# Reordering the head of a hybrid attention layer: constants on a second queue, the modulation row spread by products, other filler products

## The chip, the cores and the metric

The kernel runs on one core of one Trainium2 chip. The metric is the device time of one execution in microseconds (us); less is better. The core has a matrix engine (PE, with its weight loads shown as PEld), a vector engine (DVE), an activation engine (ACT), a small general engine (POOL) and a queue engine (SP) that issues most transfers. ACT can issue transfers too.

## The reference

One layer of a decoder with 512 positions, width 1024 and heads of 64. What matters here is its beginning:

```
mod = silu(c) @ w_ada + b_ada ;  shift, scale, gate = split(mod, 3)
h    = rms_norm(x, norm_gain) * (1 + scale) + shift
proj = h @ w_in                      # q, k, v, z of two head groups
...                                  # sliding-window group A, three-branch sparse group B
out  = x + gate * (y @ w_out)
```

`c` is one vector of 1024, `x` is 512 x 1024. The row sums of `x*x` give one factor for each position; `silu(c) @ w_ada` gives a scale and a shift for each of the 1024 channels. Both are wanted before the first product `h @ w_in`.

## The kernel before, in words

`x` lies transposed in eight tiles `xT[k]` of 128 channels by 512 positions. For each tile k the kernel needs the two columns `AB[:, k, :]` (scale and shift of its 128 channels) and the positions' factor spread over the partitions (`rbp` in PSUM, `rb` in SBUF). Then `h = A*(xT*rb) + B` is made as a high part `hh` and a low part `hl` (rounded value and remainder), the weights `w_qkv_a` of the tile likewise (`swh`, `swl`), and `first_proj(k, n)` (L281) adds three products, n = 0, 1, 2: hh by swh, hh by swl, hl by swh. Each is eight matmuls, so a tile is 24, all adding to the same six PSUM banks `sq` and `skv`.

The scale and shift come in two ways. For tiles 0 and 1 (`PE_MODS`) the matrix engine makes them: `mod_pe(k)` (L225) multiplies the columns of `w_ada` by `scz`, which holds silu(c) by column; ACT copies the result to `macc`, `mod_col(k)` (L246) sums it over the partitions by two one-column products with `ones`, and `mod_ab(k)` (L252) adds the constants on DVE. For tiles 2 to 7 the vector engine makes them: `mod_rows(k)` (L219) multiplies the rows of `w_ada` by `scrow`, silu(c) spread over all partitions, and sums along the row: two instructions of 1024 elements for a tile.

The order of the head is written by hand. Everything from L290 to L413 stands in one block (`in_order`, L66) that holds each engine's instructions, and those of each queue, in the order in which they are traced. In that order:

- SP issues `xT[0..7]` (L297), then `first` (c by column, the biases, the norm gain and the identity, 84 KB), `bias` (38 KB), then for each of four tiles the `w_ada` part in two halves (L205, L209) and the `w_qkv_a` part (L213). Behind tile 0 comes `scrow` (L305): the row `c` read 128 times, 512 KB. Then `rest`.
- PE: 20 products over zeros (`dummies`, L310), the one-column row sums of the first half of x (L330), four zero products, the row sums of the second half, the product `pl` (L343) that makes the bias line, two zero products, `mod_pe(0)`, four transposes that spread the factor `rx` (L352), two zero products, `mod_col(0)`, three zero products, `first_proj(0, 0)`.
- ACT: squares of the eight tiles (the last in two halves), tanh of c's column (L334), two copies for the bias line (L345, L346), the copy of `macc`, `weights_high(0)`, hh of tile 0 in two halves, `rb`, hf, `weights_high(1)`, and the tanh of `scrow` (L373).
- DVE: the sums of the squares (L327), silu(c) by column (L335, L336), the inverse root of eight small instructions (`rsqrt`, L97), three small products of constants, the scaling of tile 0, `mod_ab(0)`, `weights_low(0)`, the scaling of tile 1, `hl` of tile 0, `weights_low(1)`, and the product that finishes silu(c) in `scrow` (L376).

Then the loop over the tiles (L389). `new_tile(k + 1)` (L378) is traced after the second of the three products of tile k: on ACT hh, hf and the next tile's high weights; on DVE `mod_rows(k + 2)`, hl, the next tile's scaling and its low weights. `mod_pe(1)` stands behind `first_proj(0, 0)`, `mod_col(1)` and `mod_ab(1)` behind `first_proj(0, 1)`. After the loop come the other projections, attention and the output product, in which PE has most of the time.

The ring `ada_ring` and the ring `wst_ring` have four slots each; the bias line is written to DRAM (`line_d`, L348) and read back after the loop (L811).

Of the kernel before, what the change touches and what calls it, by code (L numbers as in the profile page):

```python
# [32 lines left out]
ND = (20, 2, 2, 3, 4)  # L33
# [48 lines left out]
def hybrid_layer_kernel(ctx, tc, A, out):  # L82
# [11 lines left out]
    def T2(dt, name):  # L94
        return t2.tile([128, S], dt, name=name, tag="t2")
# [26 lines left out]
    DVE.memset(ones, 1.0)  # L122

# [76 lines left out]
    def load_ada(k):  # L200
        t = ada_ring[:, k % NR]
        if k < PE_MODS:
            ada[k] = t.rearrange("p (a b c) -> p a b c", a=8, b=2)
            for e in range(2):
                SP.dma_start(ada[k][:, 4 * e:4 * e + 4], A["w_ada_cols"][k][:, 4 * e:4 * e + 4])  # L205
        else:
            ada[k] = t.rearrange("p (a b) -> p a b", a=2)
            for e in range(2):
                SP.dma_start(ada[k][:, e], A["w_ada_rows"][k - PE_MODS][:, e])  # L209
# [9 lines left out]
    def mod_rows(k):  # L219

        for e, (factor, start) in enumerate(((0.5, prm[:, k:k + 1]), (prmg[:, 8 + k:9 + k], prmg[:, k:k + 1]))):
# [3 lines left out]
    def mod_pe(k):  # L225

        pm = ps_pj.tile([128, 512], F32, name="pj")[:, 0:256]
        for j in range(8):
            c = j % 4
            PE.matmul(pm[32 * c:32 * c + 32, :], scz[:, j, :], ada[k][:, j].rearrange("p a b -> p (a b)"),  # L230
                      start=j < 4, stop=j >= 4, skip_group_check=True)
        macc[k] = stp.tile([128, 2, 128], F32, name="macc0", bufs=2)
        ACT.activation(macc[k].rearrange("p a b -> p (a b)"), pm, AF.Copy)
# [56 lines left out]
    with in_order(tc) as begun:  # L290
# [4 lines left out]
        POOL.memset(lsb[0:8, 0:LINE - NEAR], BIG)  # L295
        for k in range(8):
            SP.dma_start(xT[k], A["xT"][k])  # L297
        SP.dma_start(first, A["first"])
        SP.dma_start(bl, A["bias"])
        for k in range(NR):  # L300
            load_ada(k)
            load_wst(k)
            if k == 0:
                src = A["c"]
                SP.dma_start(scrow, bass.AP(tensor=src.tensor, offset=src.offset, ap=[[0, 128], [1, D]]))  # L305
# [4 lines left out]
        def dummies(n):  # L310
            for _ in range(n):
                PE.matmul(pj_kv[0].rearrange("p a b -> p (a b)"), zero[:, 0:128], zero, start=True, stop=True)

        dummies(ND[0])
# [3 lines left out]
        pl = pj_q[1][0:40, 0:NEAR]  # L318
        th = con.tile([128, 8], F32, name="th")
        for k in range(8):  # L320
# [3 lines left out]
            for c in (halves if k == 7 else [slice(0, S)]):  # L324
# [3 lines left out]
            if k % 4 == 3:  # L328
                for tb in range(NB):
                    PE.matmul(pr[:, tb:tb + 1], sacc[:, tb * 128:(tb + 1) * 128], ones, start=k == 3 and tb == 0,  # L330
                              stop=k == 7 and tb == NB - 1, skip_group_check=True)
            if k == 3:
                dummies(ND[4])
        ACT.activation(th, cT, AF.Tanh, scale=0.5)  # L334
        DVE.scalar_tensor_tensor(sc_col, th, 1.0, cT, op0=OP.add, op1=OP.mult)  # L335
        DVE.tensor_scalar(scz[:, :, 0], sc_col, 0.5, None, op0=OP.mult)  # L336
# [6 lines left out]
        PE.matmul(pl, bl[:, NEAR:NEAR + 40], bl[:, 0:NEAR], start=True, stop=True)  # L343
        dummies(ND[1])
        ACT.copy(lsb[0:40, LINE - NEAR:LINE], pl)  # L345
        ACT.copy(lsb[32:40, 0:LINE - NEAR], lsb[32:40, LINE - NEAR:LINE - NEAR + 1].to_broadcast([8, LINE - NEAR]))  # L346
        for a in range(2):
            SP.dma_start(line_d[a], lsb[32 * a:32 * a + 8, :])  # L348
        mod_pe(0)
# [3 lines left out]
        dummies(ND[2])  # L353
        mod_col(0)
        dummies(ND[3])
# [13 lines left out]
        weights_high(1)  # L369
        weights_low(1)  # L370
        throw = T2(F32, "throw"), T2(F32, "throw")
        for e in range(2):
            ACT.activation(throw[e], scrow[:, 512 * e:512 * e + 512], AF.Tanh, scale=0.5)  # L373
        for e in range(2):
            v = scrow[:, 512 * e:512 * e + 512]
            DVE.scalar_tensor_tensor(v, throw[e], 1.0, v, op0=OP.add, op1=OP.mult)  # L376

        def new_tile(k):  # L378

            h_high(k, halves if k < 4 else (slice(0, S),))  # L380
            if k < 7:
                mod_rows(k + 1)
# [6 lines left out]
        for k in range(8):  # L389
# [632 lines left out]
def _layout(inp):  # L1022
# [51 lines left out]
    a["c"] = cc(g("c").reshape(1, D))  # L1074
# [17 lines left out]
```

## Time and profile before

| | us |
|---|---|
| median of 3 runs | 318.29 (316.89 to 318.58) |
| profiled execution | 317.4 |
| its span, from the first to the last instruction | 315.6 |
| first product of the projection (PE L286) | 17.63 from the span's start |
| first product behind the tile loop (PE L469) | 54.18 from the span's start |
| PE busy | 307.2 (97%) |
| DVE busy | 237.4 (75%) |
| ACT busy | 195.7 (62%) |

The time is that of a whole execution and the span is what the profiler sees of it, 1.8 us less here. Busy is the time in which an engine has an instruction in work. The ends of matmuls are modelled and overlap, so the distance from one start to the next is the better price of one.

### The profile page before, as it was taken

What the parts mean: (1) busy time and instruction counts of PE and PEld (TensorE: products, weight loads), DVE (VectorE), ACT (ScalarE), POOL (GpSimd) and SP (SyncE); (2) the same over time, 40 slices, a digit from 0 to 9 for tenths busy, and PEclk for the clock granted to TensorE, in tenths of its full rate; (3) what the DMA queues carried; (4) which work ended last, traced back from release to release, by engine and by line L of the source; (5) the groups of instructions that cost most, each with busy time, mean ns of one, the idle gap of its engine ahead of it and who ended that gap; (6) DMA issues with size and microseconds to landing.
All of it is one profiled execution on the core that took longest, in us unless ns stands there. A gap on an engine that the chain in (4) does not pass through costs nothing.

```text
span 315.6 us, 5830 instructions
## 1 busy us (share of the span) xinstructions
PE 307.2 (97%) x2122; PEld 252.3 (80%) x2122; DVE 237.4 (75%) x658; ACT 195.7 (62%) x472; POOL 3.9 (1%) x21
## 2 busy tenths in 40 slices
PE   8899999999999999999999999999999999999995
PEld 3468888788988999889883888878788878788885
DVE  3589999999967558898997998988686777544221
ACT  5476557668967675676927767778785777513000
POOL 0000000000000000000000000000000000000000
PEclk9799999999999999999999999999999999999999
DMA  7999967900291908170553004222320210242201
GB/s 241 380 412 411 405 233 197 340 11 0 62 345 35 293 5 251 51 266 2 175 177 145 5 2 133 69 66 70 134 69 0 69 66 3 74 159 98 104 33 69
DMA packets 28232, 44.65 MB, mean 141 GB/s; under 512 B 1787, under 2 KB 19612, under 8 KB 28204
## 3 DMA queue, kind: packets, MB, share of 16 engines
q1 hardware_dynamic: 27052, 42.18, 39.4%
q10 hardware_dynamic: 1152, 2.10, 2.0%
q8 instruction: 17, 0.28, 0.4%
q14 instruction: 11, 0.09, 0.1%
HBM read 42.13 MB, written 2.14 MB: 140 GB/s over the span
## 4 chain that ended last, share of the span: by engine, by line
PE 79%; DVE 10%; ACT 6%; DMA 2%; issue 1%; SPq 1%; POOL 0%; ACTq 0%; DVEq 0%; POOLq 0%
PE pj L469 29%; PE pj L459 9%; PE sq L286 8%; PE po L930 7%; PE s L855 7%; PE pt L913 4%; PE skv L287 4%; PE pt L903 3%; PE s L588 3%; DVE qs L520 2%; DMA xTp<-in_xT 2%; DVE kTb L538 1%; PE po L936 1%; DVE raw L690 1%; DVE wl L174 1%
## 5 line engine op out<-in xcount | busy, mean ns | idle before, releaser
L173 ACT ACTIVATE wh<-raw 128x512 fp32r<-128x512 f32 (+1 forms) x52 | 31.2, 637 | 13.5 <-PE pj L469 13.4
L174 DVE TENSOR_TENSOR wl<-raw,wh 128x512 fp32r<-128x512 f32 (+1 forms) x52 | 34.8, 689 | 5.2 <-ACT wh L173 3.5
L459 PE MATMUL pj<-wh,hh 128*128 128x256 f32 (+1 forms) x128 | 37.0, 289 | 0.0
L459 PE MATMUL pj<-wl,hh 128*128 128x256 f32 (+1 forms) x128 | 36.7, 287 | 0.1
L459 PE MATMUL pj<-wh,hl 128*128 128x256 f32 (+1 forms) x128 | 36.6, 286 | 0.0
L867 ACT ACTIVATE pp<-pp,nm 128x256 f32<-128x256 f32 (+2 forms) x48 | 29.3, 614 | 6.6 <-DVE nm L860 6.4
L469 PE MATMUL pj<-hh,wh 128*128 128x512 f32 x80 | 32.1, 402 | 0.0
L469 PE MATMUL pj<-hh,wl 128*128 128x512 f32 x80 | 32.0, 400 | 0.0
L469 PE MATMUL pj<-hl,wh 128*128 128x512 f32 x80 | 31.8, 398 | 0.0
L860 DVE CUSTOM_DVE_ANT_0 pp<-s,bias 128x256 f32<-128x256 f32 (+2 forms) x48 | 25.5, 551 | 3.6 <-PE s L855 3.5
L469 PE MATMUL pj<-yl,wh 128*128 128x512 f32 (+1 forms) x72 | 26.6, 372 | 0.0
L469 PE MATMUL pj<-yh,wh 128*128 128x512 f32 (+1 forms) x72 | 26.6, 371 | 0.0
L469 PE MATMUL pj<-yh,wl 128*128 128x512 f32 (+1 forms) x72 | 26.4, 369 | 0.0
L1018 DVE SCALAR_TENSOR_TENSOR fin<-pj,gate,xr 128x512 f32<-128x512 f32 (+1 forms) x9 | 6.2, 691 | 25.1 <-PE pj L469 25.1
L459 PEld LDWEIGHTS pj<-wl,hh 128*128 128x128 f32 x128 | 24.1, 188 | 0.4 <-DVE wl L174 0.3
L459 PEld LDWEIGHTS pj<-wh,hh 128*128 128x128 f32 x128 | 24.1, 188 | 0.3 <-issue 0.2
L459 PEld LDWEIGHTS pj<-wh,hl 128*128 128x128 f32 x128 | 24.1, 188 | 0.2 <-issue 0.2
L855 PE MATMUL s<-kTb,qs 128*128 128x256 f32 (+2 forms) x96 | 23.5, 356 | 0.0
L888 DVE TENSOR_SCALAR pp<-pp,rr,grev 128x256 f32<-128x256 f32 (+2 forms) x48 | 21.1, 475 | 0.7
L914 ACT COPY ptT<-pt 128x384 f32<-128x384 f32 (+1 forms) x32 | 15.7, 531 | 7.0 <-PE pt L913 6.7
L904 ACT COPY ptT<-pt 128x512 f32<-128x512 f32 (+1 forms) x28 | 15.5, 552 | 5.2 <-PE pt L903 4.9
L469 PEld LDWEIGHTS pj<-hh,wh 128*128 128x128 f32 x80 | 15.0, 188 | 3.9 <-issue 1.2
(232 smaller groups left out, 709.2 us busy)
## 6 DMA issues: line engine op xcount, KB each, us to landing
ada_ring<-in_w_ada_rows SPq DMA_DIRECT2D x12, 512.0 KB, 9.3
raw<-in_w_cmp SPq DMA_DIRECT2D x8, 512.0 KB, 6.4
raw<-in_w_gate SPq DMA_DIRECT2D x8, 512.0 KB, 5.0
raw<-in_w_o SPq DMA_DIRECT2D x8, 512.0 KB, 3.8
wst_ring<-in_w_qkv_a SPq DMA_DIRECT2D x8, 384.0 KB, 9.3
xTp<-in_xT SPq DMA_DIRECT2D x8, 256.0 KB, 4.7
ada_ring<-in_w_ada_cols SPq DMA_DIRECT2D x4, 512.0 KB, 7.1
bias<-line_d SPq DMA_DIRECT2D x8, 256.0 KB, 3.4
```

Of the source, the lines that this page charges most:

```text
L173: ACT.activation(wh, src, AF.Copy)
L174: DVE.tensor_tensor(wl, src, wh.bitcast(F32), op=OP.subtract)
L286: PE.matmul(pj_q[tb], lt, w[:, 0:512], start=f, stop=l, skip_group_check=True)
L459: PE.matmul(bank[:, t * n:(t + 1) * n], h[:, tb * 128:(tb + 1) * 128], w[:, k % 2, :], start=k == 0 and m == 0, stop=k == 7 and m == 2)
L469: PE.matmul(bank, w, h[:, tok], start=k == 0 and m == 0, stop=k == 7 and m == 2)
L855: PE.matmul(ps, qs[h][:, 128 * i:128 * i + 128], k[:, hl_, lo:lo + w], start=hl_ == 0, stop=hl_ == 1)
L860: DVE.tensor_tensor_reduce(out=P[:, g, 0:w], in0=ps, in1=bt, scale=1.0, scalar=init, op0=OP.add, op1=OP.min, accum_out=nm[:, g:g + 1])
L867: ACT.activation(P[:, g, 0:e], P[:, g, 0:e], AF.Exp, bias=nm[:, g:g + 1], scale=-1.0, accum_out=dn[:, g:g + 1])
L888: DVE.tensor_scalar(v, v, rr[:, g:g + 1], gates[:, g, br:br + 1], op0=OP.mult, op1=OP.mult)
L904: ACT.copy(T[:, :, 0:nb, :], rev(pt[:, 0:2 * nb * 128].rearrange("p (g b q) -> p g b q", g=2, b=nb)))
L914: ACT.copy(T[:, 0:nb, :], rev(pt[:, 0:nb * 128].rearrange("p (b q) -> p b q", b=nb)))
L930: PE.matmul(o[64 * g:64 * g + 64, 128 * i:128 * i + 128], vb[:, 64 * g:64 * g + 64], sl["T"][g][:, b, :], start=first_of and b == 0, stop= ...
```

## The change

- `first` is issued by ACT, ahead of everything on that engine, and no more by SP. `bias` moves behind the `w_ada` part of tile 0. That part comes in three pieces (4, 2 and 2 of its eight blocks) and not two. `scrow` is not loaded any more.
- The tanh of c's column and silu(c) by column move ahead of the squares. Two diagonal tiles are made on DVE (`ident` times silu(c)'s columns, 128 x 512 each), and PE multiplies each by a 128 x 128 tile of ones: each row of the result is silu(c) (times two). ACT copies it from PSUM to `scrow` behind the squares. The tanh and the product on `scrow` go.
- Products that only fill (`fillers`, before `dummies`): 11 over zeros at the start (before 20); one of 128 columns over `xT[k]` for k = 4 to 7 and two over the squares of the first half of tile 7 (the six small ones); one over zeros behind the second row sums, one inside `mod_pe(0)`, three behind `pl`.
- The row sums of the first half of x move on PE behind the filler of k = 4. `pl` moves behind `mod_col(0)` and to bank `sq3`; its copy on ACT moves behind hh of tile 0; the second bias copy and the two transfers to `line_d` move behind `mod_pe(1)`.
- `weights_high(1)` and `weights_low(1)` move behind `first_proj(0, 0)`. The first of the two `mod_rows` instructions of tile 2 moves ahead of `mod_ab(1)`, behind `weights_low(1)`.

```diff
-ND = (20, 2, 2, 3, 4)
+ND = (11, (0, 0, 0, 0, 1, 1, 1, 1), (2, 0), 1, 1, 0, 3)
...
+    ones_sq = con.tile([128, 128], F32, name="ones_sq")
+    POOL.memset(ones_sq, 1.0)
...
-            for e in range(2):
-                SP.dma_start(ada[k][:, 4 * e:4 * e + 4], A["w_ada_cols"][k][:, 4 * e:4 * e + 4])
+            for e, n in ((0, 4), (4, 2), (6, 2)) if k == 0 else ((0, 4), (4, 4)):
+                SP.dma_start(ada[k][:, e:e + n], A["w_ada_cols"][k][:, e:e + n])
...
+        ACT.dma_start(first, A["first"])
         for k in range(8):
             SP.dma_start(xT[k], A["xT"][k])
-        SP.dma_start(first, A["first"])
-        SP.dma_start(bl, A["bias"])
         for k in range(NR):
             load_ada(k)
+            if k == 0:
+                SP.dma_start(bl, A["bias"])
             load_wst(k)
-            if k == 0:
-                src = A["c"]
-                SP.dma_start(scrow, bass.AP(tensor=src.tensor, offset=src.offset, ap=[[0, 128], [1, D]]))
...
+        def fillers(n, over=None):
             for _ in range(n):
+                l, m = (zero[:, 0:128], zero) if over is None else (over[:, 0:128], over[:, 128:256])
+                PE.matmul(pj_kv[0].rearrange("p a b -> p (a b)")[:, 0:m.shape[1]], l, m, start=True, stop=True)
+        fillers(ND[0])
+        th = con.tile([128, 8], F32, name="th")
+        ACT.activation(th, cT, AF.Tanh, scale=0.5)
+        DVE.scalar_tensor_tensor(sc_col, th, 1.0, cT, op0=OP.add, op1=OP.mult)
+        for e in range(2):
+            diag = T2(F32, "diag").rearrange("p (j q) -> p j q", j=4)
+            DVE.tensor_tensor(diag, ident[:, None, :].to_broadcast([128, 4, 128]),
+                              sc_col[:, 4 * e:4 * e + 4][:, :, None].to_broadcast([128, 4, 128]), op=OP.mult)
+            PE.matmul(pj_q[e], ones_sq, diag.rearrange("p j q -> p (j q)"), start=True, stop=True)
+        DVE.tensor_scalar(scz[:, :, 0], sc_col, 0.5, None, op0=OP.mult)
...
-        pl = pj_q[1][0:40, 0:NEAR]
+        pl = pj_q[3][0:40, 0:NEAR]
...
+            fillers(ND[1][k], xT[k])
+            if k == 4:
+                sums(sacc_a, True, False)
...
+                if k == 7:
+                    fillers(ND[2][n], sq[:, c])
...
+        sums(sacc, False, True)
+        for e in range(2):
+            ACT.activation(scrow[:, 512 * e:512 * e + 512], pj_q[e], AF.Copy)
...
-        PE.matmul(pl, bl[:, NEAR:NEAR + 40], bl[:, 0:NEAR], start=True, stop=True)
-        dummies(ND[1])
-        ACT.copy(lsb[0:40, LINE - NEAR:LINE], pl)
-        ACT.copy(lsb[32:40, 0:LINE - NEAR], lsb[32:40, LINE - NEAR:LINE - NEAR + 1].to_broadcast([8, LINE - NEAR]))
-        for a in range(2):
-            SP.dma_start(line_d[a], lsb[32 * a:32 * a + 8, :])
-        mod_pe(0)
+        fillers(ND[3])
+        mod_pe(0, lambda: fillers(ND[4]))
+        fillers(ND[5])
...
-        dummies(ND[2])
         mod_col(0)
-        dummies(ND[3])
+        PE.matmul(pl, bl[:, NEAR:NEAR + 40], bl[:, 0:NEAR], start=True, stop=True)
+        fillers(ND[6])
...
+        ACT.copy(lsb[0:40, LINE - NEAR:LINE], pl)
         ACT.activation(rb, rbp, AF.Copy)
...
-        weights_high(1)
-        weights_low(1)
-        throw = T2(F32, "throw"), T2(F32, "throw")
-        for e in range(2):
-            ACT.activation(throw[e], scrow[:, 512 * e:512 * e + 512], AF.Tanh, scale=0.5)
-        for e in range(2):
-            v = scrow[:, 512 * e:512 * e + 512]
-            DVE.scalar_tensor_tensor(v, throw[e], 1.0, v, op0=OP.add, op1=OP.mult)
...
-                mod_rows(k + 1)
+                mod_rows(k + 1, (1,) if k == 1 else (0, 1))
...
                 if k == 0 and n == 0:
+                    weights_high(1)
                     mod_pe(1)
+                    weights_low(1)
+                    mod_rows(2, (0,))
+                    ACT.copy(lsb[32:40, 0:LINE - NEAR], lsb[32:40, LINE - NEAR:LINE - NEAR + 1].to_broadcast([8, LINE - NEAR]))
+                    for a in range(2):
+                        SP.dma_start(line_d[a], lsb[32 * a:32 * a + 8, :])
```

## Rows read from the trace of the kernel before

**Rows 1.** The page: TensorE's granted clock in 40 equal slices of the span (tenths of full speed, 7.9 us a slice), and the engines' shares of the chain that ended last.

```profile
PEclk9799999999999999999999999999999999999999
PE 79%; DVE 10%; ACT 6%; DMA 2%; issue 1%; SPq 1%; POOL 0%; ACTq 0%; DVEq 0%; POOLq 0%
```

**Rows 2.** Busy time in stretches (us from the span's start): the stretch, its length, then busy us and instructions of PE, PEld, DVE, ACT and POOL, then the granted clock of TensorE (1.00 is 2.4 GHz, 0.50 is 1.2 GHz), the busy share of the transfer engines and GB/s.

```profile
1.20:5.20 4.00, 3.97 (x10) 1.46 (x11) 0.77 (x3) 2.07 (x3) 0.00 (x0) 1.00 0.79 216
3.40:4.40 1.00, 1.00 (x4) 0.38 (x3) 0.00 (x0) 0.98 (x2) 0.00 (x0) 1.00 0.74 125
5.40:7.60 2.20, 2.20 (x11) 0.84 (x9) 1.19 (x2) 1.63 (x3) 0.00 (x0) 1.00 1.04 397
7.00:7.50 0.50, 0.50 (x4) 0.10 (x1) 0.40 (x1) 0.34 (x2) 0.00 (x0) 1.00 1.04 402
8.50:10.50 2.00, 1.29 (x8) 0.55 (x7) 1.76 (x4) 1.45 (x4) 0.00 (x0) 1.00 1.04 294
12.00:12.50 0.50, 0.50 (x2) 0.13 (x2) 0.40 (x4) 0.26 (x1) 0.00 (x0) 0.57 1.06 428
12.50:13.00 0.50, 0.50 (x2) 0.00 (x0) 0.43 (x3) 0.47 (x2) 0.00 (x0) 0.50 1.04 420
15.00:15.50 0.50, 0.50 (x7) 0.50 (x4) 0.00 (x0) 0.38 (x1) 0.00 (x0) 0.52 1.00 410
15.50:16.00 0.50, 0.50 (x5) 0.37 (x4) 0.11 (x1) 0.49 (x1) 0.00 (x0) 1.00 1.04 424
27.00:45.20 18.20, 18.20 (x101) 15.20 (x100) 18.20 (x30) 10.18 (x16) 0.00 (x0) 1.00 1.00 378
```

**Rows 3.** The chain of waits that ended last, in order of time, from the last tile of x to the first product of the projection: start us, us, what.

```profile
4.02 5.26 DMA xTp<-in_xT
...
9.30 0.72 ACT sq L325 x2
...
10.13 0.42 DVE sacc L327
...
10.60 1.05 PE pj L330 x8
11.65 0.56 PE sq L343 x2
12.21 0.97 PE skv L312 x2
13.18 1.86 PE pj L230 x16
15.04 0.82 PE pj L352 x4
15.86 0.43 PE skv L312 x2
16.29 0.35 PE pj L250 x4
...
16.74 0.22 DVE AB L256
...
16.98 0.61 ACT hh L363
...
17.63 0.50 PE sq L286
```

**Rows 4.** Instructions of PE in order of time: start us, us, engine, line, operation, out<-in, partitions x elements, count, and in brackets the idle time before and its releaser.

```profile
10.60 1.05 PE L330 MATMUL pj<-ones,sacc 128*128 128x1 f32 x8 [0.81 <-DVE sacc L327]
...
19.22 1.07 PE L230 MATMUL pj<-ada_ring,scz 128*32 128x256 f32 x16
...
23.57 0.39 PE L286 MATMUL sq<-swh,hh 128*128 128x512 f32 x1
...
62.84 0.66 PE L514 MATMUL pt<-first,qn 128*128 128x128 f32 x4
```

**Rows 5.** The same of DVE.

```profile
13.27 0.16 DVE L108 SCALAR_TENSOR_TENSOR n_y<-n_t,n_y 128x4 f32<-128x4 f32 x1
...
20.03 0.96 DVE L265 TENSOR_TENSOR swl<-wst_ring,swh 128x768 fp32r<-128x768 f32 x1
20.90 1.29 DVE L376 SCALAR_TENSOR_TENSOR scrow<-throw,scrow 128x512 f32<-128x512 f32 x2
...
22.46 1.27 DVE L222 CUSTOM_DVE_ANT_0 ada_ring<-ada_ring,scrow,first 128x1024 f32<-128x1024 f32 x1
...
23.66 1.34 DVE L222 CUSTOM_DVE_ANT_0 ada_ring<-ada_ring,scrow,prmg 128x1024 f32<-128x1024 f32 x1
...
24.93 0.69 DVE L279 TENSOR_TENSOR hl<-hf,hh 128x512 fp32r<-128x512 f32 x1
```

**Rows 6.** The same of ACT.

```profile
3.42 1.25 ACT L325 ACTIVATE sq<-xTp 128x512 f32<-128x512 f32 x2 [1.40 <-DMA xTp<-in_xT]
...
12.24 0.36 ACT L345 COPY raw<-sq 40x256 f32<-40x256 f32 x1 [2.12 <-PE sq L343]
...
23.64 1.08 ACT L276 ACTIVATE hf<-xTp,AB 128x256 f32<-128x256 f32 x2
```

**Rows 7.** The issue of the second half of `w_ada` for tile 0 (SP, L205): duration ns min/median/max, first and last start us; and the time from issue to landing.

```profile
L205 SPq DMA_DIRECT2D ada_ring<-in_w_ada_cols x1: 327/327/327, 6.4 to 6.4; - x1
...
DMA to landing us min/median/max: 6.5/6.5/6.5
```

More of the change, by code (lines that the diff above doesn't have):

```diff
@@ L217, in hybrid_layer_kernel, with mod_rows, mod_pe @@
     AB = con.tile([128, 8, 2], F32, name="AB")
-    def mod_rows(k):
-        for e, (factor, start) in enumerate(((0.5, prm[:, k:k + 1]), (prmg[:, 8 + k:9 + k], prmg[:, k:k + 1]))):
+    def mod_rows(k, es=(0, 1)):
+        for e in es:
+            factor, start = ((0.5, prm[:, k:k + 1]), (prmg[:, 8 + k:9 + k], prmg[:, k:k + 1]))[e]
             DVE.tensor_tensor_reduce(out=ada[k][:, e], in0=ada[k][:, e], in1=scrow, scale=factor, scalar=start,
                                      op0=OP.mult, op1=OP.add, accum_out=AB[:, k, 1 - e:2 - e])
-    def mod_pe(k):
+    def mod_pe(k, between=lambda: None):
         pm = ps_pj.tile([128, 512], F32, name="pj")[:, 0:256]
@@ L229, in mod_pe @@
             c = j % 4
+            if j == 4:
+                between()
             PE.matmul(pm[32 * c:32 * c + 32, :], scz[:, j, :], ada[k][:, j].rearrange("p a b -> p (a b)"),
@@ L295, in hybrid_layer_kernel, with sums @@
         POOL.memset(lsb[0:8, 0:LINE - NEAR], BIG)
+        ACT.dma_start(first, A["first"])
         for k in range(8):
             SP.dma_start(xT[k], A["xT"][k])
-        SP.dma_start(first, A["first"])
-        SP.dma_start(bl, A["bias"])
         for k in range(NR):
             load_ada(k)
+            if k == 0:
+                SP.dma_start(bl, A["bias"])
             load_wst(k)
-            if k == 0:
-                src = A["c"]
-                SP.dma_start(scrow, bass.AP(tensor=src.tensor, offset=src.offset, ap=[[0, 128], [1, D]]))
         SP.dma_start(rest, A["rest"])
         DVE.memset(scz, 0.0)
-        def dummies(n):
+        def fillers(n, over=None):
             for _ in range(n):
-                PE.matmul(pj_kv[0].rearrange("p a b -> p (a b)"), zero[:, 0:128], zero, start=True, stop=True)
-        dummies(ND[0])
+                l, m = (zero[:, 0:128], zero) if over is None else (over[:, 0:128], over[:, 128:256])
[10 more added lines that the diff above has]
+        DVE.tensor_scalar(scz[:, :, 0], sc_col, 0.5, None, op0=OP.mult)
         halves = [slice(0, 256), slice(256, 512)]
         pr = ps_pj.tile([128, 512], F32, name="pj")
-        pl = pj_q[1][0:40, 0:NEAR]
-        th = con.tile([128, 8], F32, name="th")
+        pl = pj_q[3][0:40, 0:NEAR]
+        def sums(acc, f, l):
+            for tb in range(NB):
+                PE.matmul(pr[:, tb:tb + 1], acc[:, tb * 128:(tb + 1) * 128], ones, start=f and tb == 0,
+                          stop=l and tb == NB - 1, skip_group_check=True)
         for k in range(8):
@@ L323, in hybrid_layer_kernel @@
                 sacc = sq
-            for c in (halves if k == 7 else [slice(0, S)]):
+            fillers(ND[1][k], xT[k])
+            if k == 4:
+                sums(sacc_a, True, False)
+            for n, c in enumerate(halves if k == 7 else [slice(0, S)]):
                 ACT.activation(sq[:, c], xT[k][:, c], AF.Square)
@@ L327, in hybrid_layer_kernel @@
                     DVE.tensor_tensor(sacc[:, c], sacc[:, c], sq[:, c], op=OP.add)
[L328 to L331, printed above, removed]
+                if k == 7:
+                    fillers(ND[2][n], sq[:, c])
             if k == 3:
[L333 to L336, printed above, removed]
+                sacc_a = sacc
+        sums(sacc, False, True)
+        for e in range(2):
+            ACT.activation(scrow[:, 512 * e:512 * e + 512], pj_q[e], AF.Copy)
         sx = con.tile([128, NB], F32, name="sx")
@@ L1073, in _layout @@
     a["bias"] = bias
-    a["c"] = cc(g("c").reshape(1, D))
     return a
```

## The prediction

> **What bounds the kernel now.** I read the page first: PE has 79% of the chain that ended last, and the clock line falls below 9 in one slice only, the second, 7.9 to 15.8 us [rows 1]. So PE's work sets the time, and whatever keeps PE from its first projection product is paid in full. That product starts at 17.63. Second, the chain of waits of the head [rows 3]: the last tile of x lands at 9.28, squares and vector sum take it to 10.55, the row sums to 11.65, and from there the chain stays on PE's own list until the spread of rx ends at 15.86: `pl` 0.56, two zero products 0.97, `mod_pe(0)` 1.86, transposes 0.82. The reader should see that nobody waited for that list's data: rx was ready at 13.43 [rows 5], 1.6 us before the transposes began. Third, the stretches [rows 2]: the granted clock goes to 0.57 in the half us from 12.0, is 0.50 (1.2 GHz) at 12.5, 0.52 from 15.0 and 1.00 (2.4 GHz) from 15.5. Before it fell PE had run one-column row sums and four zero products and had stood 0.81 us idle [rows 4]. `mod_pe(0)` thus took 1.86 where `mod_pe(1)`, at full clock, takes 1.07 [rows 4]. Fourth, the tile loop: from 27.0 to 45.2 DVE is busy 18.20 of 18.20 us [rows 2]. There the vector chain sets the pace, so what the head saves is kept only if that chain starts earlier by as much.
>
> **The list between row sums and spread.** Call the delay of x's last tile D (below). The row sums end at 11.65 + D. `pl` and two zero products leave this place; one zero product stands ahead of `mod_pe(0)` and one in it. A zero product costs 0.2 at full clock (11 in 2.20) and 0.4 at half (10 in 4.00) [rows 2]. If the clock holds, PE needs 0.2 + 1.07 + 0.2 = 1.47 and is free at 13.1 + D. rx comes at 13.43 + D: the vector engine's eight small steps now end last and PE waits 0.3. Four transposes take 0.66 at full clock [rows 4]: spread done at 14.15 + D, against 15.86.
>
> **From the spread to the first product.** Two zero products (0.43) go. `mod_col(0)` takes 0.35, and from its end to the first product the chain has 17.63 - 16.64 = 0.99 [rows 3], unchanged: 15.5 + D. But PE now has `pl` (0.56) and three zero products (0.6) behind `mod_col`: 14.5 + 1.16 = 15.65 + D. The ends are close; I take 15.6 + D.
>
> **The delay D.** The trace has no `first` ahead of x. Its transfer, 84 KB, must share the transfer engines with x. Lower end: in 3.4 to 4.4 the engines are busy only 0.74 and move 125 GB/s, so part or all may fit there: D = 0. By bytes alone, at the 402 GB/s of 7.0 to 7.5, it is 0.2. Upper end: in 8.5 to 10.5, where `first` and the bias (38 KB) passed, 294 GB/s were moved; 2 us at a shortfall of 108 GB/s is 0.54 us, with their own bytes (0.30) 0.84, of which `first` has 128 of 161 rows: 0.65 [rows 2]. I take 0.45, nearer the upper end because that row is this very transfer.
> The Trainium skill, page "DMA: Bandwidth & Descriptors", section "Issuing engines are not separate DMA queues", speaks against this edit: transfers issued by different engines end on the same 16 transfer engines and interleave, and a second issuer saves only issue time. By it D is the whole occupancy; by the row of 3.4 to 4.4 it can be nothing, and the gain would be 0.45 larger.
> What the move buys is that c's column is early; that was not on the chain.
>
> **Moved ahead of the row sums, at no cost while covered.** Tanh before the squares: cover is ACT's idle time. It waited 1.40 for the first tile; the seven squares ahead of the last tile need 7 x 0.63 = 4.4 [rows 6], so they must begin by 4.9 + D; beyond that each us is a us. Two diagonal tiles on DVE, about 1.29 (two of 512 columns [rows 5]), lie where DVE waits for squares. On PE eleven zero products end near 5.7. The two products with ones have 512 columns; nearest is `pl`, 256 columns for 0.56: 2.2 together, to 7.9. Then come filler, first row sums (1.05), three fillers of at most 0.28 each, the last of them waiting for x's last tile, and two behind the first half's square: about 10.7, ahead of the 11.0 at which the last sum can start. The cover is 0.3 us at full clock and gone at half. The two `scrow` copies lie in ACT's idle time behind the squares; it next worked at 12.24 [rows 6].
>
> **Loads.** The second half of `w_ada` landed at 6.4 + 6.5 = 12.9 [rows 7]. `mod_pe(0)` reaches its later blocks at 12.8 + D, so the finer pieces wait at most 0.1, under rx's cover. Without `scrow`, 512 KB, all later loads come about 1.3 us earlier at 402 GB/s, which keeps step with engines that are 1.6 us earlier. On SP's queue the line transfers now stand behind the loads of tile 4 and wait for ACT's late copy; behind them are loads of tile 5, wanted ten us later, and the line is read after the loop: nothing.
>
> **The vector chain in tiles 0 and 1**, in us from the first product. Before: low weights of tile 1 at 2.40, `scrow` 3.27 to 4.56, `mod_ab(1)`, row sums of tile 2 at 4.83 and 6.03, hl of tile 1 at 7.30 [rows 5]. After: on ACT one more copy (0.36 [rows 6], about 0.3 of it net) stands ahead of the high weights of tile 1, so the low weights start at 2.7; steps of 0.87 and 1.20 (starts in [rows 5]) bring `mod_ab(1)` to 4.8, 0.2 later than before. hf of tile 1, which ended at 24.72 with hl starting at 24.93, ends 0.2 later: hl at 7.3, as before. So the 1.29 us that DVE loses in work turn into idle time in front of hl. PE asked for tile 1 at 5.94 [rows 4], hh is there at 5.8. The loop, and all behind it, shifts by what the first product shifts.
>
> **Sum.** First product at 15.6 + 0.45 = 16.05 instead of 17.63: 1.6 us off (2.0 with D = 0, 1.4 with D = 0.65). Of that about 0.8 is `mod_pe(0)` at full clock, the rest `pl` and zero products that left the path, less D. The profiled execution took 317.4, with a span of 315.6, so 315.8. It lies 0.9 under the median of the runs shown and inside their spread; the mean of these four executions is 317.8, and the sum from there is 316.2, my prediction.
>
> **Rivals.**
> *The clock falls all the same* (0.25). For: from 7.9 to 12 PE has little but one-column sums and small fillers, four zero products fewer than before, and before it fell after such a stretch. Against: its gaps are at most 0.3 to 0.5, not 0.81. Then: row sums end at 12.1, zero product 0.4, `mod_pe(0)` 1.86 with one of 0.4 inside, transposes 0.82: 15.6; then 0.35 and 0.99 to 1.2: first product at 17.1, 0.5 us off: 317.3.
> *The vector chain gives part back* (0.12). The early row sum of tile 2 now holds up `mod_ab(1)`, and with it hh, hf and hl of tile 1. If low weights or w_ada's rows of tile 2 are late by 0.8, hl comes at 8.1, and DVE, which has no idle time up to 45.2, never makes it up: 317.0. For: DVE's full row. Against: 1.0 us of idle time in front of hl covers the second row sum, not the first.
> *More than forecast* (0.10). D near 0, and ordinary runs that suffer more from the low clock than the profiled one: 2.0 from the median or more, near 315.4.
> *Slower: the constants come late* (0.08). Tanh heads ACT's list. If the 84 KB get through only behind x, at 9.3 + 0.2, ACT starts the squares at 9.7, seven and two halves (4.4 + 0.72) end at 14.8 instead of 10.02: 4.8 late, less the 2.0 that the list gives: 320.6. It decides from a landing at 4.9 on, and turns the sign from 6.9. Against: x's eight transfers are issued one by one over 3.7 us, so `first` is not behind all of them.
> By the Trainium skill, same page, section "Queues, rings and completion order", each transfer engine takes turns between the queues, which also speaks against it; no run here shows it.
>
> **How the numbers follow.** The forecast has 0.45; its own range is 315.3 to 317.0 (D from 0 to 0.65, and the two bases 0.4 apart). A measurement of this kernel can tell about 0.5% from no change, 1.6 us: faster means under 316.7. Of the forecast's 0.45 some 0.36 lie there, with 0.10 of the larger gain and 0.04 of the vector and clock cases: 0.50. Slower than 319.9: the late constants and a remainder of the clock case, if the full list before the row sums also runs at 1.2 GHz: 0.10. The rest, 0.40, is the same. The range leaves out the late constants above and the far end of the larger gain below: 314.9 to 318.2.
>
> **What would show it.** Right: granted clock 1.00 from 8 to 17; `mod_pe(0)` near 1.3 with its filler; PE idle about 0.3 in front of the transposes, released by DVE L108; x's last tile landing 0.2 to 0.65 later; first product near 16.05; DVE idle some 1.0 in front of hl of tile 1; the first L469 product 36.5 us behind the first projection product, as before. Wrong: a clock of 0.50 somewhere in 9 to 16; ACT's first square behind 4.9; low weights of tile 1 later than 2.8 from the first product; or a gap between first product and loop end that is not 36.5.

## The result, and the profile after

Over nine executions each, the kernel before took 317.9 us (median; 316.89 to 319.15) and the kernel after 315.65 (315.07 to 317.42): ratio 0.9931, 95% interval 0.9907 to 0.9955, 2.2 us less. The prediction was 316.2, so the time came out as forecast. The terms of its sum did not: what the head lost in time comes mostly from the clock and little from the shorter list, and it reaches the end only because the load of `scrow` is gone.

The profiled execution of after took 316.46 us with a span of 314.7, and the clock fell in it. First its busy time by stretches, the columns as in [rows 2]:

```profile
3.40:4.40 1.00, 1.00 (x4) 0.39 (x3) 0.22 (x2) 0.50 (x2) 0.00 (x0) 1.00 1.05 408
8.50:10.50 2.00, 2.00 (x18) 1.81 (x17) 1.79 (x4) 1.97 (x5) 0.00 (x0) 1.00 0.96 287
11.00:11.50 0.50, 0.50 (x4) 0.22 (x3) 0.16 (x1) 0.00 (x0) 0.00 (x0) 0.82 1.06 412
12.00:12.50 0.50, 0.50 (x8) 0.00 (x0) 0.41 (x3) 0.00 (x0) 0.00 (x0) 0.50 1.02 363
14.50:15.00 0.50, 0.50 (x6) 0.50 (x5) 0.00 (x0) 0.50 (x2) 0.00 (x0) 0.77 0.94 373
26.00:44.20 18.20, 18.20 (x101) 15.19 (x101) 18.20 (x29) 10.17 (x17) 0.00 (x0) 1.00 0.97 366
```

The reader is to see a granted clock of 0.50 at 12.0, with 0.82 in the half us from 11.0 and 0.77 in that from 14.5: by these shares it fell near 11.3 and rose near 14.7, some 0.75 us earlier than in before (12.1 and 15.5), although PE was busy 2.00 of 2.00 us from 8.5. DVE is still full for 18.20 us of the tile loop. Now PE in order of time in the same execution, the columns as in [rows 4]:

```profile
11.53 1.08 PE L235 MATMUL pj<-ada_ring,scz 128*32 128x256 f32 x8
13.08 1.08 PE L235 MATMUL pj<-ada_ring,scz 128*32 128x256 f32 x8 [0.47 <-issue]
14.09 0.95 PE L367 MATMUL pj<-first,n_y 128*128 128x128 f32 x4
...
15.86 0.82 PE L316 MATMUL skv<-zero 128*128 128x512 bf16 x3
16.39 0.53 PE L291 MATMUL sq<-swh,hh 128*128 128x512 f32 x1
```

The first product stands at 16.39 instead of 17.63 [rows 3]. The same kernel profiled again (experiment `e10_after`, 315.29 us) kept the clock:

```profile
11.43 0.64 PE L235 MATMUL pj<-ada_ring,scz 128*32 128x256 f32 x8
12.00 0.39 PE L316 MATMUL skv<-zero 128*128 128x512 bf16 x1
12.32 0.98 PE L235 MATMUL pj<-ada_ring,scz 128*32 128x256 f32 x8
13.23 0.65 PE L367 MATMUL pj<-first,n_y 128*128 128x128 f32 x4
...
14.88 0.82 PE L316 MATMUL skv<-zero 128*128 128x512 bf16 x3
15.40 0.53 PE L291 MATMUL sq<-swh,hh 128*128 128x512 f32 x1
```

Here the first product is at 15.40, the low clock's price in the head of this kernel being 1.0. Tile 1's first product comes at 22.34 and 21.37 in the two, 5.95 and 5.97 behind tile 0's. In `e10_after` the head's gain reaches the end whole: beside the profile of before the first product is 2.23 earlier, the first product behind the tile loop 2.21 (51.97 and 54.18), the end of the span 2.2 (313.4 and 315.6). ACT's and DVE's rows of the first of the two, the profile of after (columns as in [rows 6] and [rows 5]):

```profile
3.90 0.21 ACT L320 ACTIVATE th<-first 128x8 f32<-128x8 f32 x1 [1.45 <-DMA first<-in_first]
4.02 1.70 ACT L346 ACTIVATE sq<-xTp 128x512 f32<-128x512 f32 x3
```

```profile
21.33 1.33 DVE L225 CUSTOM_DVE_ANT_0 ada_ring<-ada_ring,scrow,prmg 128x1024 f32<-128x1024 f32 x1
22.59 0.08 DVE L225 DVE_READ_ACCUMULATOR2_ANT AB<- 128x1 f32 x1
23.56 0.69 DVE L284 TENSOR_TENSOR hl<-hf,hh 128x512 fp32r<-128x512 f32 x1 [0.89 <-ACT hf L281]
```

The constants landed at 3.88, and the 1.29 us that DVE no longer spends on `scrow` [rows 5] became 0.89 us idle in front of the h rest of tile 1.

The time follows the clock of the head, which every execution shows as a mean over its span. Of 111 executions of the kernel before in the experiments' batches, 15 had a mean granted clock of 0.998 or more (median 316.82), 53 had 0.994 to 0.995 (317.68), 42 had 0.989 (319.40) and one 0.993. Of 21 of after, 17 had 0.998 or more (315.45) and 4 had 0.995 (316.46 to 317.42). No profile of before at full clock exists. Runs are compared below within one level of that mean; "at full clock" means 0.998 or more.

### The profile page after: what moved, and what is told of

It reads as the page before. It is cut to its first block, busy times and chain, and to the rows that moved or that the text cites. A ratio compares the mean times of both kernels' runs of the same rounds, so it can differ in the third digit from the quotient of the medians.

```text
span 314.7 us, 5828 instructions
## 1 busy us (share of the span) xinstructions
PE 306.3 (97%) x2122; PEld 252.9 (80%) x2123; DVE 237.3 (75%) x658; ACT 195.5 (62%) x472; POOL 5.1 (2%) x22
## 4 chain that ended last, share of the span: by engine, by line
PE 77%; DVE 12%; DMA 4%; ACT 3%; issue 2%; SPq 0%; POOL 0%; DVEq 0%; ACTq 0%; POOLq 0%
PE pj L483 29%; PE sq L291 7%; PE po L944 7%; PE s L869 7%; PE pj L473 7%; PE pt L927 4%; PE skv L292 4%; DMA raw<-in_w_gate 3%; PE pt L917 3%; PE s L602 3%; DVE qs L534 2%; DVE kTb L552 1%; DVE wl L176 1%; PE po L950 1%; DVE raw L704 1%
## 5 line engine op out<-in xcount | busy, mean ns | idle before, releaser
L473 PE MATMUL pj<-wh,hl 128*128 128x256 f32 (+1 forms) x128 | 36.5, 285 | 0.0
L918 ACT COPY ptT<-pt 128x512 f32<-128x512 f32 (+1 forms) x28 | 15.5, 552 | 5.1 <-PE pt L917 4.9
```

Source lines behind the costliest of these rows:

```text
L473: PE.matmul(bank[:, t * n:(t + 1) * n], h[:, tb * 128:(tb + 1) * 128], w[:, k % 2, :], start=k == 0 and m == 0, stop=k == 7 and m == 2)
L918: ACT.copy(T[:, :, 0:nb, :], rev(pt[:, 0:2 * nb * 128].rearrange("p (g b q) -> p g b q", g=2, b=nb)))
```

## Experiments

**First: which part carries the gain?** The kernel before again, and three with one part each.

`e1_before`: no edit. 

> The kernel before once more, for the mean granted clock of each of its runs (0.995 where the clock fell for 3.4 us in the head, 1.000 where it did not) and for a second profile. Theory A (mine: PE's list between row sums and spread, plus the clock in part of the runs): the clock falls in nearly all runs of the kernel before, as against 4 of 9 of the changed kernel, so that the clock makes about 0.5 of the 2.2 us and the list the rest. Rival B (the clock alone): it falls in all runs of before, and the runs of the changed kernel in which it fell (316.5 to 317.4) are then no faster than before: before should show 316.5 to 317.4 too. Rival C (the clock has no part): it falls in before as seldom as in the changed kernel, about 4 in 9, and runs of before at 1.000 lie near 317.0. On the transfers: if x's last tile landing at 9.28 in the first profile was chance, this profile has another value, between 8.6 and 9.6.

Measured: 317.9, ratio 0.9995 (0.9969 to 1.0021); no execution at full clock, 8 of 12 at 0.994 or 0.995, 4 at 0.989. So the clock falls more often than in after, where it fell in three of nine (not four, as the expectation has it): rival C is out. Rival B is out as well: before takes 317.68 with one fall, after 316.46 to 317.42. x's last square began at 9.04 in this profile.

`e2_before_fill`:

```
-ND = (20, 2, 2, 3, 4)
+ND = (20, 2, 2, 3, 8)
```

> The kernel before with 8 in place of 4 zero products behind the first row sums, which fill the 0.81 us in which PE stood idle ahead of the second row sums. Theory A: the clock then holds in most runs; mod_pe(0), two zero products and transposes are at 2.4 GHz, which is 0.8 + 0.5 + 0.2 less on PE's list: first product at 16.2 instead of 17.6 and 1.0 to 1.5 us less than before, about 316.6. Rival B (the clock alone makes the gain): 2.2 less, as the changed kernel. Rival C (the clock has no part): within 0.3 us of before.

Measured: the clock stayed up in all 12, yet 317.36, ratio 0.9966 (0.9944 to 0.9989). The head did gain: first product at 16.55. But tile 1 came at 23.41, 6.86 us behind it and not 5.94 [rows 4]. The profile's ACT rows and waits (columns: engine, line, waited for, us in total, times, longest) name why:

```profile
19.26 0.85 ACT L262 ACTIVATE swh<-wst_ring 128x768 fp32r<-128x768 f32 x1 [1.08 <-DMA wst_ring<-in_w_qkv_a]
20.01 1.13 ACT L373 ACTIVATE throw<-scrow 128x512 f32<-128x512 f32 x2
```

```profile
DVE swl L265 <- ACT swh L262: 1.2, 1, 1.2
ACT hh L276 <- DVE AB L256: 1.2, 1, 1.2
ACT swh L262 <- DMA wst_ring<-in_w_qkv_a: 1.1, 1, 1.1
```

ACT stands 1.08 us waiting for the weights of tile 1, whose transfer is issued behind the 512 KB of `scrow`. In the kernel before, with its clock low in the head, ACT starts that step at 19.16 without a wait:

```profile
19.16 0.83 ACT L262 ACTIVATE swh<-wst_ring 128x768 fp32r<-128x768 f32 x1
```

The slow head had hidden this transfer; when exactly it landed there, that trace does not record.

`e3_before_list`:

```
-        PE.matmul(pl, ...)  dummies(ND[1])  ACT.copy(lsb..., pl) ... line_d stores
         mod_pe(0)
...
-        dummies(ND[2])
         mod_col(0)
+        PE.matmul(pl, ...)
```

> The kernel before with PE's list alone changed: the bias product moved behind mod_col(0) with three zero products behind it, its copies where the changed kernel has them, and the two pairs of zero products ahead of mod_pe(0) and ahead of mod_col(0) left out. Theory A: PE's list loses 0.56 + 0.97 + 0.43 = 1.96 at the low clock; then mod_pe(0) starts at 11.7 + and has to wait for the last of w_ada's blocks (landed at 12.9), so the transposes start near 13.9 instead of 15.0: 1.0 to 1.5 us less than before. Rival B (the clock alone): within 0.4 us of before, or slower, as four filling products are gone. Rival C: all of the 2.2 us.

The copies and stores of the bias line stand where the kernel after has them.

Measured: slower, 319.37, ratio 1.0035 (1.0009 to 1.006); 7 of 12 at 0.984, 4 at 0.988 or 0.989, 1 at 0.995 (316.77). In the profile PE waited 1.32 us ahead of the second row sums, and the clock was low from 11.1 to 21.4 (columns as in [rows 2]):

```profile
8.50:10.50 2.00, 0.75 (x4) 0.13 (x2) 1.64 (x4) 1.45 (x4) 0.00 (x0) 1.00 0.96 286
11.00:11.50 0.50, 0.50 (x5) 0.50 (x4) 0.14 (x1) 0.00 (x0) 0.00 (x0) 0.64 1.04 424
20.50:21.00 0.50, 0.50 (x9) 0.27 (x12) 0.50 (x2) 0.00 (x0) 0.00 (x0) 0.50 1.04 408
```

The transposes did come earlier (13.82 instead of 15.04 [rows 3]), but all that follows ran at half clock, the first product at 17.41. At an equal level of the clock the short list is the faster one: 316.77 (one run) against 317.68 at 0.995, 318.65 (median of the four) against 319.40 at 0.989. It loses because its clock falls in all twelve, and in seven of them to a mean of 0.984, which before never shows. The shorter list alone is no gain: it needs the denser feeding.

`e4_before_first`:

```
+        ACT.dma_start(first, A["first"])
         for k in range(8):
             SP.dma_start(xT[k], A["xT"][k])
-        SP.dma_start(first, A["first"])
```

> The kernel before with one edit: the constants (first) are issued by ACT ahead of x and no more by SP behind x. It measures the delay D of x's last tile by itself. As forecast: x's last tile lands 0.2 to 0.65 later than 9.28 and the kernel is 0.2 to 0.65 us slower. Rival: D is 0 or less, as the changed kernel's profile has x's last tile at 8.8; then the kernel is within 0.2 us of before or faster by up to 0.4.

Measured: 317.55, ratio 0.9996 (0.9964 to 1.0027); 5 of 12 at full clock, their median 316.75 beside 316.82 of before. In the profile (316.72, at full clock) the last square of x began at 8.76 instead of 9.30 [rows 3], so x was not delayed. PE's list there is that of before, `pl` and all zero products in it, at full clock:

```profile
9.97 1.05 PE L330 MATMUL pj<-ones,sacc 128*128 128x1 f32 x8 [0.45 <-DVE sacc L327]
10.95 0.62 PE L343 MATMUL sq<-raw 33*40 33x256 f32 x2
11.50 0.60 PE L312 MATMUL skv<-zero 128*128 128x512 bf16 x2
12.04 1.10 PE L230 MATMUL pj<-ada_ring,scz 128*32 128x256 f32 x16
13.07 0.65 PE L352 MATMUL pj<-first,n_y 128*128 128x128 f32 x4
...
15.50 0.50 PE L286 MATMUL sq<-swh,hh 128*128 128x512 f32 x1 [0.34 <-ACT hh L363]
```

```profile
18.23 0.85 ACT L262 ACTIVATE swh<-wst_ring 128x768 fp32r<-128x768 f32 x1 [1.10 <-DMA wst_ring<-in_w_qkv_a]
```

The first product stood at 15.50, and still tile 1 came 6.89 behind it, ACT having waited 1.10 for its weights. Beside the profile of before, whose clock fell, the first product is 2.13 earlier, tile 1 1.18, and the end of the span 0.7.

**Second: fillers, the early row sum, the load.**

`e5_after_nosmall`:

```
-ND = (11, (0, 0, 0, 0, 1, 1, 1, 1), (2, 0), 1, 1, 0, 3)
+ND = (11, (0, 0, 0, 0, 0, 0, 0, 0), (0, 0), 1, 1, 0, 3)
```

> The kernel after without its six small fillers (four in the squares, two in front of the second row sums). Theory A (they keep the granted clock up through the head): the clock falls in nearly every execution, mean granted clock 0.989 to 0.995, and the median moves from 315.65 to 316.5 to 317.4, as the three of nine executions of the kernel after that showed 0.995. Rival (they do nothing, the shorter list does it): 315.5 to 315.8 and the clock at 1.000 in two of three executions as before the cut; the six cost 0.1 us at most, so nothing can be won either.

Measured: 318.47; one execution of 12 at full clock (315.5), 3 at 0.995, 8 at 0.989 or 0.984 (318.29 to 319.6). The six small fillers decide how often the clock holds (1 of 12 without them, 17 of 21 with them), and without them the mean falls further than expected.

`e9_after_dense`:

```
+            if k == 4:
+                fillers(3)
             if k == 4:
                 sums(sacc_a, True, False)
```

> The kernel after with three full zero products more ahead of the first row sums. Theory A (granted clock follows how thinly TensorE is fed between 7.5 and 11 us): mean clock 0.998 to 1.000 in all executions, none above 316.0, median 315.3 to 315.5. Rival (the clock falls at random, or the fall in a third of the executions comes from the stretch behind the second row sums): still a third of the executions at 0.995 and 316.5; the median as before, 315.6.

Measured: 315.51 (315.11 to 316.06), all six at full clock, ratio 0.9895 (0.987 to 0.992). `e10_after`, the kernel after again in a later batch: 

> The kernel after, unchanged, again: how often its clock falls where the kernel before's fell in nearly all executions (in half of them for twice as long). Theory A (the list of after keeps the clock up only just, the extra products of the dense version do it for good): times between 315.1 and 315.7 at a mean clock of 0.998 to 1.000, 316.3 to 317.4 at 0.995, both present; ratio to before 0.990 to 0.994. Rival (it holds the clock as well as the dense version): 315.1 to 315.9 in all.

Measured: 315.44 (314.9 to 316.77), 11 of 12 at full clock, ratio 0.9924 (0.9899 to 0.9949). At full clock the dense version is no faster (315.5 beside 315.43), and its six executions, beside 17 of 21 of after, do not show that it holds the clock more often.

`e6_after_rows`, both row sums of tile 2 behind AB:

```
-                mod_rows(k + 1, (1,) if k == 1 else (0, 1))
+                mod_rows(k + 1)
...
-                    mod_rows(2, (0,))
```

> The kernel after with both row sums of tile 2 behind tile 1's AB again. Theory A (the forecast's neutral vector chain; the h rest of tile 1 waits for ScalarE's fp32 h, 0.89 us idle in the profile after): one row sum (0.66 us) more ahead of that rest fits into the 0.89 us, so 315.6, within 0.3 of the kernel after, and VectorE's idle ahead of the rest of tile 1 falls from 0.89 to 0.2. Rival (the row sum moved forward is worth its time): 0.6 us slower, 316.2 to 316.3, with the rest of tile 1 0.6 later.

Measured: 318.13; at full clock 317.05 (7 of 12), the other five at 0.983 or 0.984 and 320.4 to 321.3: far above both expectations (whose 0.66 for a row sum is wrong as well: it takes 1.2). `e7_after_load`, the same with the loaded row back (its edit on top of `e6` is that of `e12` below): 

> The kernel before this one in the list (both row sums behind AB) with the loaded row of c back: its 512 KB broadcast behind tile 0's weights, tanh and product on ScalarE and VectorE behind tile 1's weights; the two copies from PSUM are out, the products of ones times diagonal tiles still run. Theory B (new: the loads of tile 1 behind the 512 KB set when tile 1 can begin once the head is shorter): the product of ones still stands at 15.5 (16.4 where the clock falls), but ScalarE waits about 1 us for tile 1's weights, tile 1's first product comes 6.7 to 6.9 us behind tile 0's instead of 5.95, and the time is 0.8 to 1.2 us over the kernel after: 316.5 to 316.9. Forecast's step (the removal of the load is worth nothing): tile 1 5.95 us behind tile 0, and 315.6 to 315.9.

Measured: 316.89; at full clock 316.78 (5 of 8), so no dearer than `e6` and against theory B as put. The profiled execution had a low clock up to 21.3 and could not show the wait. Both had to be asked again with the clock held.

**Third: the same two with the dense fill.** `e11_dense_rows` is `e9` with the edit of `e6`: 

> The dense version (after with three zero products more, 315.5, clock never down) with both row sums of tile 2 behind tile 1's AB again, so that the clock plays no part. Theory A (forecast: this part is neutral, the rest of tile 1 has slack of about 0.9 us): 315.4 to 315.8, tile 1's first product 5.95 to 6.0 us and its rest 7.2 to 7.3 us behind tile 0's first product. Rival (the 316.6 to 316.8 that this edit showed at full clock without the dense fill is its price): 316.5 to 316.8, with the rest 0.6 later or a wait in the tile loop.

`e12_dense_load`, on top of it:

```
             load_wst(k)
+            if k == 0: SP.dma_start(scrow, <row of c, spread over 128 partitions>)
...
-        for e in range(2): ACT.activation(scrow[...], pj_q[e], AF.Copy)
...
                     weights_low(1)
+                    <tanh on ACT into throw, product on DVE into scrow, as before>
```

> The kernel before this one in the list with the loaded row of c back (512 KB behind tile 0's weights; tanh and product behind tile 1's weights; the copies from PSUM are out). Theory B (that load sets when tile 1 begins behind a head at full clock): ScalarE waits 0.8 to 1.2 us for tile 1's weights, tile 1's first product 6.7 to 6.9 us behind tile 0's, and 0.8 to 1.2 us over the kernel before this one in the list: 316.3 to 316.9. Forecast's step (the removed load is worth nothing): the same time as that kernel within 0.3, tile 1 at 5.95.

Measured: `e11` 317.04, at full clock 316.57 (7 of 12, the clock falling in the other five in spite of the dense fill); `e12` 316.84, at full clock 316.87 (11 of 12). By times alone the rival of `e11` had won and the load cost only 0.3. The profiles say otherwise. ACT and DVE in `e12`:

```profile
16.89 0.81 ACT L384 ACTIVATE hf<-xTp,AB 128x512 f32<-128x512 f32 x1
18.86 0.85 ACT L267 ACTIVATE swh<-wst_ring 128x768 fp32r<-128x768 f32 x1 [1.16 <-DMA wst_ring<-in_w_qkv_a]
```

```profile
19.73 0.96 DVE L270 TENSOR_TENSOR swl<-wst_ring,swh 128x768 fp32r<-128x768 f32 x1 [1.31 <-ACT swh L267]
20.61 1.28 DVE L418 SCALAR_TENSOR_TENSOR scrow<-throw,scrow 128x512 f32<-128x512 f32 x2
21.82 0.15 DVE L260 TENSOR_TENSOR AB<-pj,first 128x1 f32<-128x1 f32 x1
```

The same places in `e11`, without the load:

```profile
17.47 0.84 ACT L267 ACTIVATE swh<-wst_ring 128x768 fp32r<-128x768 f32 x1
20.34 0.16 DVE L260 TENSOR_TENSOR AB<-pj,first 128x1 f32<-128x1 f32 x1 [1.04 <-PE pj L255]
```

Tile 1 came 6.98 us behind the first product (22.78 and 15.80), in `e11` 5.98 (21.66 and 15.68): theory B's wait, the distance a little over the 6.7 to 6.9 expected. By the end of the tile loop `e12` stood 1.43 behind `e11`. And `e11` lost its time elsewhere: by the end of the tile loop it stood 0.34 behind `e10`, by 168 us about 1.0. Its loads of later weights (SP: duration ns, first and last start us), here beside those of `e9`, first `e9`, then `e11`:

```profile
L157 SPq DMA_DIRECT2D raw<-in_w_kv_sel x2: 540/1136/1732, 34.8 to 45.3; - x2
```

```profile
L157 SPq DMA_DIRECT2D raw<-in_w_kv_sel x2: 540/585/630, 45.9 to 46.4; - x2
```

The first half of `w_kv_sel` is issued 11 us later. My explanation, which no trace shows by itself, is that the builder hands out the buffers of these weights by its own reckoning of when they come free, and that the moved row sum changed that reckoning: the same loads in the same order, waiting for other buffers. By the time of that issue, 34.5 to 39.0, `e12` and all other kernels here but `e6` (46.4) have the rotation of the kernel before (36.5). ACT's splits of later weights follow suit, as at 155 us, again `e9` and then `e11`:

```profile
155.35 1.14 ACT L175 ACTIVATE wh<-raw 128x512 fp32r<-128x512 f32 x2
```

```profile
156.80 0.63 ACT L175 ACTIVATE wh<-raw 128x512 fp32r<-128x512 f32 x1 [0.53 <-PE pj L484]
159.60 0.63 ACT L175 ACTIVATE wh<-raw 128x512 fp32r<-128x512 f32 x1 [2.17 <-PE pj L484]
```

`e13_rows_memset` tests it: on top of `e11` it puts a piece of work of 0.48 us into the place on DVE that the row sum had, which brings the old rotation back:

```
                     weights_low(1)
+                    junk = T2(F32, "throw")
+                    DVE.memset(junk[:, 0:512], 0.0)
```

> The dense version with both row sums of tile 2 behind tile 1's AB, as in the kernel that took 316.45 to 316.9 at full clock, and one clearing of a 128x512 scratch tile on VectorE in the place that the row sum had (VectorE idles 1.04 us there). With it the builder hands out the buffers of the later weights in the same rotation as in the dense version, where without it SyncE issued the first half of w_kv_sel at 45.85 instead of 34.8 and ScalarE's splits of later weights waited for other buffers. Theory A (the place of the row sum is worth nothing, the other rotation of buffers took the 1.1 us): 315.3 to 315.8, first half of w_kv_sel issued near 35, rest of tile 1 7.2 to 7.3 us behind the first product. Rival (the place of the row sum is worth 1 us through VectorE): 316.4 to 316.9 in spite of the old rotation.

Measured: 315.7 (315.48 to 316.81), at full clock 315.66 (6 of 7); the first half of `w_kv_sel` issued at 35.3, and in the profile (clock low in the head) the rest of tile 1 at 23.82, 7.32 behind the first product:

```profile
20.18 0.48 DVE L413 MEMSET throw<- 128x512 f32 x1
21.15 0.16 DVE L260 TENSOR_TENSOR AB<-pj,first 128x1 f32<-128x1 f32 x1 [0.48 <-PE pj L255]
...
22.55 1.34 DVE L225 CUSTOM_DVE_ANT_0 ada_ring<-ada_ring,scrow,prmg 128x1024 f32<-128x1024 f32 x1
23.82 0.69 DVE L284 TENSOR_TENSOR hl<-hf,hh 128x512 fp32r<-128x512 f32 x1
```

Theory A: the place of the row sum is worth about 0.15 (315.66 beside 315.5), less than the spread, the other rotation cost 0.9 (316.57 - 315.66). And with equal rotation and equal clock, the loaded row with its tanh and product costs 316.87 - 315.66 = 1.2. These differences are between medians of groups at full clock, some from different batches; the spread within a group is 0.5 to 1.7 us.

## Why the prediction was right, and which step was wrong

The measured gain in one chain, all from medians: the kernel before with its usual one fall of the clock 317.68; the clock kept, 316.82 (0.86 less); all of after but the removed load and the early row sum, clock kept (`e12`), 316.87 (nothing); the load with its tanh and product out (`e13`), 315.66 (1.2); the early row sum, 315.5 (0.15). Another order would share it out otherwise: the load alone taken out of before was not run.

The forecast for the time was right, in part by luck. It had 1.6 us off the first product; the profile at full clock has 2.2, and these reached the end, as was said of the loop. But the clock was booked at half its price, the list at two to six times its own, and D at 0.45 where no delay was seen: the errors cancelled in part.

- **"About 0.8 is `mod_pe(0)` at full clock": right for `mod_pe(0)`, half of what the clock is worth in the head.** In the chain of `e4`, read as [rows 3], `mod_pe(0)` takes 1.03 instead of 1.86. But the two zero products ahead of it fall from 0.97 to 0.54 as well, and the transposes from 0.82 to 0.59. From the start of the second row sums to the first product before needs 7.03 us and `e4`, its list unchanged, 5.53 (`e2`: 5.51): 1.5. That 0.86 of it shows in the time of before is another number, that of a kernel in which tile 1 waits for its weights. How often was left out as well: before had full clock in 15 of 111 executions and the longer fall (a mean of 0.989) in 42, which costs another 1.7.
- **"The rest `pl` and zero products that left the path": mis-sized, 0.2 to 0.65 in place of 1.25** (0.8, and the 0.45 of D that it had to pay for). From the start of the second row sums to the first product the six profiles of the short list at full clock need 4.87 to 5.32, `e4` and `e2` with the old list 5.5; the first product stands at 15.40 in `e10` and at 15.50 in `e4`. What left the path was long because the clock was low: where the clock falls, the short list is worth 0.75 to 0.9 (`e3`, at equal level). At the kept clock, with the load in place, it is worth nothing at the end: `e4` with the old list and `e12` with the short one take 316.75 and 316.87. Moved without the fill it is a loss, by the clock that falls with it (`e3`).
- **"Without `scrow` ... keeps step": held in the kernel after, but the gain hangs on it, and the sum gave it no term.** Without the load tile 1 comes 5.95 to 5.98 and the loop end 36.4 to 36.6 behind the first product, in seven profiles. With the load and the clock kept, its weights could be split only at 18.2 to 19.3 (`e4`, `e12`, `e2`), just when the slow head of before wanted them (19.16, no wait): tile 1 comes 6.86 to 6.98 and the loop end 37.6 to 37.9 behind. So the removed load is what lets the head's gain pass, 1.2 at full clock. The runs take the load out together with its tanh and product. The traces point to the load: in before the tanh and product stand without a wait ahead of them, and `mod_ab(1)` begins 4.63 behind the first product (22.26), as in `e11` with neither (4.66); in `e12`, behind the wait of 1.16, it begins at 6.02. Not run, and so open: the old list with the clock kept and the load out. An estimate from what the list saved in the head is 0.2 to 0.65 us behind after.
- **D, taken as 0.45: no delay was seen.** x's last square began at 8.83 in after and at 8.76 in `e4`, against 9.30 in before. Single profiles scatter, though: 8.76 to 9.50 in the ten with `first` on ACT, 9.04 to 9.67 in the four with it behind x. The time of `e4` at full clock is that of before within 0.1. The row that pulled D up, 294 GB/s from 8.5 to 10.5, is no mark of `first`: after has 287 there without it. And the row of 125 GB/s from 3.4, which pulled it down, was a single reading: 264 to 371 in the other three profiles that issue `first` behind x. By the Trainium skill, page "DMA: Bandwidth & Descriptors", section "Issuing engines are not separate DMA queues", a second issuer saves issue time only; that agrees with `e4`, in that no time came from it.
- **A zero product "0.4 at half (10 in 4.00)": misread.** The granted clock in that row is 1.00. At 0.50 two of them took 0.97 [rows 3]; why the first ten of the kernel take 0.4 each at a granted 1.00 no run shows.
- **Squares, tanh, diagonals covered: right.** Constants landed at 3.88, well ahead of the 4.9 at which they would have cost; the slower rival did not occur.
- **PE idle 0.3 for rx: once.** In `e9` the transposes waited 0.23 behind the inverse root. In `e10` rx was ready at 13.04 and PE came at 13.23: the second half of `mod_pe(0)` took 0.98 instead of 0.64, having waited for the last piece of `w_ada`, for which the forecast had 0.1 at most.
- **PE's own list binding at 15.6 + D against 15.5 + D: open.** With the clock kept the first product follows the end of its h half and overlaps the fillers' rows; no run took those three products away.
- **Vector chain neutral: right.** Rest of tile 1 at 7.17 (after), 7.31 (`e10`), 7.33 (`e11`), 7.32 (`e13`) behind the first product, 7.30 before. The rival of the vector chain didn't occur.
- **Rival "the clock falls all the same", 0.25 and 317.3:** it occurred in 4 of 21 executions, at 316.46 to 317.42, the profiled one among them, where the sign "a clock of 0.50 somewhere in 9 to 16" so stood. The first product came at 16.39 there, not at 17.1.
- **The loop end 36.5 behind the first product:** 36.42 in after, as said. Behind it 0.4 us of the profiled run's gain went: DVE waited 0.49 and 0.15 for gate weights, with kn behind it (the row below), where before had no wait at that place. The forecast had nothing for this. The earlier loop by itself is not the cause: `e9`, `e10` and `e11`, whose loops end earlier still (51.69 to 52.31 against 52.81), have no such wait, while `e1`, at 53.99, has one of 0.4. What is, stays open.

```profile
122.41 1.28 DVE L704 CUSTOM_DVE_ANT_0 raw<-raw,scrow,first 128x1024 f32<-128x1024 f32 x1 [0.49 <-DMA raw<-in_w_gate]
```

## What to carry to other kernels

When a stage is shortened, ask what becomes late next and look for it among the transfers that today arrive just in time: a wait of zero in the trace may be a wait that the slowness hides, and a load costed at nothing may be what lets the gain through. When a clock is to be won back, price the whole stretch at the higher clock first, and only then what a shorter list saves of it: here the list looked like 1.25 us and was 0.2 to 0.65. Where a builder assigns buffers by its own estimate, compare where later loads are issued before an experiment's time is put down to the edit; a neutral edit cost 0.9 us that way. And compare executions at the same granted clock: the clock's fall in the head moved single runs by 0.9 to 2.6 us, as much as the change.

## What the runs showed of the hardware that was not expected

- The granted clock fell after stretches in which PE was busy: in the profile of after at 11.3, behind 2.00 busy of 2.00 us from 8.5 (0.55 of 1.00 from 7.5), and in that of `e13` at 11.4, behind 4.00 busy of 4.00 us from 7.5, while `e10`, with 2.00 and 1.00, kept it, and `e5`, with 0.87 of 2.00, kept it in its profiled run and lost it in 11 of 12. The same program so holds or loses it from run to run; the share is what the fillers move: 15 of 111 at full clock in before and 12 of 12 with four zero products more (`e2`); 1 of 12 without the six small fillers and 17 of 21 with them. Three more zero products on top show nothing further: 6 of 6 in `e9`, but 24 of 31 in `e11`, `e12` and `e13`, which have the same fill.
- With `first` on a second issuer, the transfer engines moved 387 to 414 GB/s from 3.4 to 4.4 in ten profiles, against 125 to 371 in the four where it stands behind x. Over the four us from 1.4 the two groups overlap (261 to 298 against 229 to 279), so the bytes may only have moved to another place in time.
- `e2` took 317.36 with the clock kept, 0.5 more than before's own runs at full clock; its profile has x's last square at 9.67, but one profile doesn't settle whether that is the cause.
